# Value projections in products of 512 columns, cosine products into the rotated tiles, and four smaller moves, in a two-layer streaming encoder

## The chip, the cores and the metric

The kernel runs on one core of a Trainium2 chip. A core has a matrix engine (TensorE, PE in the profile; its weight loads are shown as PEld), a vector engine (VectorE, DVE), an activation engine (ScalarE, ACT), a general engine (GpSimd, POOL) and a queue that issues transfers (SyncE, SP). Each takes its instructions in the order in which they were written for it. Products are summed in eight banks of PSUM, each of 512 float32 columns in 128 partitions; everything else stands in SBUF or in HBM.

The metric is the device time of one execution in microseconds, as the median of several runs. Lower is better.

## The reference, cut to what matters

The input is one sequence of 1024 tokens of width 1024, float32. Layer 0 normalises, projects once, and runs two branches; layer 1 is a convolution module.

```
x = x + mixer_ab(rmsnorm(x))        # layer 0
x = x + mixer_conv(rmsnorm(x))      # layer 1
return rmsnorm(x)

mixer_ab(h):
    u, g_s5, q, k, v, g_ret = split(h @ w_in)       # 1024, 1024, 512, 512, 1024, 1024
    y_s5 = s5(u);  y_s5 = y_s5' * sigmoid(y_s5' @ glu_w + glu_b), y_s5' = gelu(y_s5)
    y_ret = retention(q, k, v)
    return concat(y_s5 * silu(g_s5), y_ret * silu(g_ret)) @ w_out

retention: 8 heads, key width 64, value width 128
    q, k = rope(q) / 8, rope(k)      # [x1 cos - x2 sin, x1 sin + x2 cos]
    scores = (q k^T) * decay mask, within chunks of 64
    out = scores v + (decayed q) S,  S = decayed sum of k v^T over earlier chunks
    out = normalised over each head's 128 columns

mixer_conv(h):
    a, b, g = split(h @ w_in)
    u = depthwise conv (31 taps) of a * sigmoid(b);  u = silu(layernorm(u)) * silu(g)
    return u @ w_out
```

## The kernel before

Activations are kept transposed: 128 features in the partitions, tokens along the free side, in halves of 512 tokens (`h` 0 and 1). To keep float32's accuracy each operand is split into a high and a low part of the type float32r. A block of eight feature tiles is then 8 x 3 products (`mm3`, lines 141 to 148): high weights by high data, high weights by low data, low weights by high data. The weights' high part is a cast on ACT (line 137), the low part a subtraction on POOL (line 138). Weights are fetched in one fixed sequence (`plan`), two ahead (`wnext`), in three buffers each for the raw, high and low parts. The weights that are used once for each half of the tokens write their low part to HBM the first time (line 112) and read it back the second time (`wload_again`, lines 115 to 124).

The data operands of a stage lie in two sets of 16 tiles, `A0` for the first half and `A1` for the second (pool `opA`). The next stage's operands take the same tiles as soon as their last reader is done.

Retention goes by pairs of heads (`retention`, line 802). For each pair `ret_proj` projects keys and queries (`project`, line 830), each as two products of 24 instructions into one of three projection banks, evacuated by DVE with the norm's factor into the tile `raw`. `turn` (line 840) rotates: four transfers exchange the 32-row blocks of `raw` into `swp`; POOL multiplies `raw` by the cosines and `swp` by the sines, both in place; DVE sums them into the rotated tile. Only the keys of pair 2 are projected ahead, before pair 1's heads.

Values have the tokens as rows, so here the data are the stationary operand and the weights are streamed. Pair 0 computes those of pairs 0 and 1 together, in products of 512 columns (`ret_values_wide`, line 887): for each half four banks (from the five auxiliary ones) are filled side by side while four pieces of the weights go by, so that each piece is loaded twice. Pairs 2 and 3 each compute their own, in products of 256 columns, one bank of 128 tokens after another (`ret_values`, line 868), with two pieces of weights.

`ret_heads` (line 909) transposes the rotated keys (`ktp`, then `kt` on DVE), forms the states (`kv`, `S`), the scores (`sp`), their masked copy (`sc`, line 959) and the output products (`ro`), takes each head's mean and variance (the root on ACT, `last_rs`), and transposes back (`rt`). Beside the retention, `y_pass` (line 779) fetches the state-space branch's output, applies Gelu on ACT and writes it to HBM (`yn_d`); the two passes of a pair stand behind the roots of the pair before on ACT. After pair 3 the GLU (lines 1055 to 1075) loads `yn_d` back (`yf`) and splits it into `yh` and `yl` (`split`, line 1016). The subtractions of the second half stand behind pair 3's `kt` on DVE.

In layer 1 the gates `silu(g)` are written to HBM (`gs_d`) and read back in `conv_norm` (line 1279, tile `gl`). The last stage, `w_out_c`, multiplies by the last weights (`woc`), adds the residual, and `final_norm` needs the sum of squares over all eight blocks (`token_sums`), its root, and a product that spreads it to all partitions (`spread`). The second half's last three blocks are done in quarters of 256 tokens; the last block's second quarter, and what follows it, is issued behind the spread of the first quarter (line 1392).

The program is written in the order of these stages, but the order on each engine is chosen beforehand by a planner that simulates the program: among what is ready it takes the lowest priority number (`at`). `issue_after(x)` keeps what is written in its block behind `x` on x's engine. So the heads of one pair are mixed with the projections of the next.

Of the kernel before, what the change touches and what calls it, by code (L numbers as in the profile page):

```python
# [11 lines left out]
F32 = mybir.dt.float32  # L12
# [26 lines left out]

class Trunk:  # L40
# [22 lines left out]
    def plan(self):  # L63

        A = self.A
        seq = [(A["w_ab"][nb], f"u{nb}") for nb in range(8)]
        seq += [(A["w_ab"][nb], f"g{nb}") for nb in range(8, 24)]
        for p in range(4):
            seq += [(A["w_ab"][28 + p], f"k{p}"), (A["w_ab"][24 + p], f"q{p}")]

            if p == 0:
                seq += [(A["w_v"][j], f"v{p}_{h}_{j}") for h in range(2) for j in range(4)]
            elif p > 1:
                seq += [(A["w_v"][2 * p + i], f"v{p}_{i}") for i in range(2)]
# [12 lines left out]
        seq += cg(1, range(G0))  # L87
        seq += [(A["w_out_c"][nb], f"woc{nb}_{h}") for h in range(2) for nb in range(8)]
        self.wseq, self.wissued, self.wgot = seq, {}, 0
        self.wnames, self.lo_d = {n for _, n in seq}, {}  # L90
# [24 lines left out]
    def wload_again(self, src, name, low):  # L115
        nc = self.nc
        wf = self.wp.tile([P, D], F32, name=f"wf_{name}", tag="wf", bufs=3)
        wh = self.wp.tile([P, KB, P], F32R, name=f"wh_{name}", tag="wh", bufs=3)
        wl = self.wp.tile([P, KB, P], F32R, name=f"wl_{name}", tag="wl", bufs=3)
# [3 lines left out]
        nc.sync.dma_start(wl[:].rearrange(fl).bitcast(F32), low)  # L123
        return wh, wl
# [663 lines left out]
    def retention(self, st):  # L788
# [13 lines left out]
        for pair in range(4):  # L802
            cur = list(ahead or self.ret_proj(pair))[-1]

            ahead = pair == 1 and self.ret_proj(pair + 1)
            if ahead:
                next(ahead)
            if pair == 0:
                V = self.ret_values_wide()
            elif pair > 1:  # L810
                V = self.ret_values(pair)
            with ExitStack() as held:
                if pair:
                    held.enter_context(self.tc.issue_after(self.last_rs.ins))
                for cb in (2 * pair, 2 * pair + 1):
                    self.y_pass(rq, cb)

            def turned():
                if pair == 3:
                    early.close()  # L820
                    self.lp = self.pool("l1", side="right")
            self.ret_heads(pair, *cur, V, turned)

    def ret_proj(self, pair):
# [5 lines left out]
        def project(nm):  # L830
            w = self.wnext(f"{nm}{pair}")
            raw = raws[nm] = self.rq.tile([P, T], F32, name=f"{nm}raw_{pair}", tag="raw", bufs=2)
            for h in range(2):
# [3 lines left out]
                last = nc.vector.tensor_tensor(raw[:, c], ps[:], self.R[:, c], op=ALU.mult)  # L837
            return last

        def turn(nm, behind=None):  # L840
# [27 lines left out]
    def ret_values(self, pair):  # L868

        nc = self.nc  # L870
        wv = [self.wnext(f"v{pair}_{i}") for i in range(2)]
        vt = self.rp.tile([P, 8, 256], F32, name=f"v_{pair}", tag="v", bufs=2)
        for b in range(8):
            ps = self.bank(f"mm_v{pair}_{b}", aux=False)
            h, o = b // 4, (b % 4) * P
            for kb in range(KB):
                xh, xl = self.xs[h][kb]
                i, k4 = kb // 4, kb % 4
                wh = wv[i][0][:].rearrange("p (k a) n -> p k (a n)", a=2)[:, k4, :]
                wl = wv[i][1][:].rearrange("p (k a) n -> p k (a n)", a=2)[:, k4, :]  # L880
                nc.tensor.matmul(ps[:, :256], xh[:, o:o + P], wh, start=kb == 0, stop=False)
                nc.tensor.matmul(ps[:, :256], xh[:, o:o + P], wl, start=False, stop=False)
                nc.tensor.matmul(ps[:, :256], xl[:, o:o + P], wh, start=False, stop=kb == KB - 1)
            nc.scalar.mul(vt[:, b, :], ps[:, :256], self.Rtok[:, b:b + 1])
        return lambda p, b, hh: vt[:, b, hh * P:(hh + 1) * P]

    def ret_values_wide(self):

        nc = self.nc
        res = []  # L890
        for h in range(2):
            vt = self.rp.tile([P, 4, HALF], F32, name=f"v_0_{h}", tag="v", bufs=2)
            pss = [self.bank(f"mm_v0_{h}_{b}") for b in range(4)]
            for j in range(4):
                wh, wl = (t[:].rearrange("p (k a) n -> p k (a n)", a=4) for t in self.wnext(f"v0_{h}_{j}"))
# [11 lines left out]
        return lambda p, b, hh: res[b // 4][:, b % 4, (2 * p + hh) * P:(2 * p + hh + 1) * P]  # L907

    def ret_heads(self, pair, K, Q, qadds, V, turned):
# [39 lines left out]

        sc = [rp.tile([P, 8, P], F32, name=f"sc{hh}_{pair}", tag=f"sc{hh}", bufs=1) for hh in range(2)]  # L950
        for hf in range(2):
# [6 lines left out]
            for hh in range(2):  # L958
                v.tensor_tensor(sc[hh][:, 4 * hf:4 * hf + 4, :], sps[hh][:].rearrange("p (b i) -> p b i", b=4),
                                self.mask[:, 2 * pair + hh, :].unsqueeze(1).broadcast_to([P, 4, P]), op=ALU.mult)  # L960
# [60 lines left out]
    def layer0_back_and_layer1(self, st):  # L1021
# [217 lines left out]
        def conv_norm(h):  # L1239
# [26 lines left out]
            for nb in range(8):  # L1266
# [12 lines left out]
                nc.sync.dma_start(g[:], self.gs_d[rows(nb), hs(h)])  # L1279
# [71 lines left out]
        for h in range(2):  # L1351
# [31 lines left out]
            with self.at(430000):  # L1383
                last = [w_out_c(h, nb, quarters) for nb in (5, 6, 7)]
# [4 lines left out]
                after = self.last_spread  # L1389
# [40 lines left out]
def layout(inp):  # L1430
# [10 lines left out]
    wv = w[:, 3072:4096].reshape(2, 4, P, 4, 256)  # L1441
    A["w_v"] = wv.transpose(3, 0, 2, 1, 4).reshape(8, P, KB, P)
    A["w_v"][:4] = w[:, 3072:3584].reshape(4, 2, P, HALF).transpose(0, 2, 1, 3).reshape(4, P, KB, P)
# [49 lines left out]
```

## Time and profile before

| | |
|---|---|
| median of 3 runs | 1215.66 us (1213.5 to 1219.05) |
| profiled execution | 1212.99 us, span of the profile 1211.2 us |
| TensorE clock granted, mean | 0.997 |
| PE busy | 1195.8 us, 99% of the span |
| DVE, POOL, ACT busy | 62%, 55%, 40% |
| value products of 512 columns, pairs 0 and 1 | 192, from 359.3 to 402.8 us |
| value products of 256 columns, pair 2 and pair 3 | 192 each, from 470.2 and from 529.5 us |
| GLU's first product | 553.3 us |

All times inside the profile are counted from the start of the span. A row of the timeline gives the start, the duration, the engine, the line, the operation with output and inputs, how many were merged and, in brackets, the idle time before it and what ended it. Matmuls overlap in the pipeline: the duration of one is longer than the distance to the next, and the distance is what a product costs.

### The profile page before, as it was taken

What the parts mean: (1) busy time and instruction counts of PE and PEld (TensorE: products, weight loads), DVE (VectorE), ACT (ScalarE), POOL (GpSimd) and SP (SyncE); (2) the same over time, 40 slices, a digit from 0 to 9 for tenths busy, and PEclk for the clock granted to TensorE, in tenths of its full rate; (3) what the DMA queues carried; (4) which work ended last, traced back from release to release, by engine and by line L of the source; (5) the groups of instructions that cost most, each with busy time, mean ns of one, the idle gap of its engine ahead of it and who ended that gap; (6) DMA issues with size and microseconds to landing.
All of it is one profiled execution on the core that took longest, in us unless ns stands there. A gap on an engine that the chain in (4) does not pass through costs nothing.

```text
span 1211.2 us, 17238 instructions
## 1 busy us (share of the span) xinstructions
PE 1195.8 (99%) x6468; PEld 1001.7 (83%) x6468; DVE 748.2 (62%) x1337; ACT 479.9 (40%) x706; POOL 664.0 (55%) x457
## 2 busy tenths in 40 slices
PE   9999999999999999999999999999999999999997
PEld 7888888888888889998888888888888788888876
DVE  7965655555412457457547102699999699899533
ACT  7212232332223233144335322545535575434652
POOL 2059988888237253253453651678453567758642
PEclk9999999999999999999999999999999999999998
DMA  9342433333385166467446877765667654356664
GB/s 334 105 140 72 140 129 132 128 128 139 110 284 177 53 208 160 155 208 256 143 158 223 285 272 250 243 209 208 212 241 256 222 192 152 123 176 240 237 254 149
DMA packets 100227, 227.11 MB, mean 188 GB/s; under 512 B 9264, under 2 KB 38192, under 8 KB 99504
## 3 DMA queue, kind: packets, MB, share of 16 engines
q1 hardware_dynamic: 100144, 226.01, 55.1%
q8 instruction: 51, 0.84, 0.3%
q14 instruction: 32, 0.26, 0.1%
HBM read 160.51 MB, written 61.28 MB: 183 GB/s over the span
## 4 chain that ended last, share of the span: by engine, by line
PE 94%; DMA 2%; ACT 2%; DVE 1%; issue 0%; SPq 0%; POOL 0%; DVEq 0%
PE mm_g L148 7%; PE mm_g L147 7%; PE mm_g L146 7%; PE mm_wo L148 5%; PE mm_wo L146 5%; PE mm_wo L147 5%; PE mm_a L148 2%; PE mm_b L147 2%; PE mm_b L148 2%; PE mm_a L146 2%; PE mm_a L147 2%; PE mm_b L146 2%; PE mm_u L148 2%; PE mm_u L147 2%; PE mm_u L146 2%; PE mm_glu L146 2%
## 5 line engine op out<-in xcount | busy, mean ns | idle before, releaser
L1194 DVE SCALAR_TENSOR_TENSOR cv<-u,convw,cv 128x512 f32<-128x512 f32 x398 | 273.5, 752 | 11.9 <-ACT cv L1180 9.6
L1174 POOL TENSOR_TENSOR tp<-tp,tp 128x512 f32<-128x512 f32 x64 | 82.9, 1296 | 45.5 <-ACT tp L1173 44.4
L148 PE MATMUL mm_g<-xh,wl_g 128*128 128x512 f32 x256 | 100.8, 394 | 0.0
L147 PE MATMUL mm_g<-xl,wh_g 128*128 128x512 f32 x256 | 100.6, 393 | 0.0
L146 PE MATMUL mm_g<-xh,wh_g 128*128 128x512 f32 x256 | 100.5, 393 | 0.0
L1173 ACT ACTIVATE tp<-u,convw 128x512 f32<-128x512 f32 x64 | 45.7, 719 | 35.6 <-POOL tp L1174 33.9
L329 DVE TENSOR_TENSOR gt<-mm_g,R 128x512 f32<-128x512 f32 x32 | 21.9, 686 | 60.0 <-PE mm_g L148 60.0
L138 POOL TENSOR_TENSOR wl_v<-wf_v,wh_v 128x1024 fp32r<-128x1024 f32 x12 | 29.0, 2425 | 51.9 <-ACT wh_v L137 51.9
L147 PEld LDWEIGHTS mm_g<-xl,wh_g 128*128 128x128 f32 x256 | 48.1, 188 | 11.3 <-issue 1.6
L148 PEld LDWEIGHTS mm_g<-xh,wl_g 128*128 128x128 f32 x256 | 48.0, 188 | 10.6
L146 PEld LDWEIGHTS mm_g<-xh,wh_g 128*128 128x128 f32 x256 | 48.1, 188 | 9.6
L148 PE MATMUL mm_oc<-zh,wl_woc 128*128 128x512 f32 (+1 forms) x152 | 54.3, 360 | 1.0 <-DMA wl_woc<-lo_woc 1.0
L1094 DVE TENSOR_TENSOR x<-mm_wo,xr 128x512 f32<-128x512 f32 x16 | 11.1, 691 | 70.3 <-PE mm_wo L148 39.6
L147 PE MATMUL mm_oc<-zl,wh_woc 128*128 128x512 f32 (+1 forms) x152 | 53.9, 357 | 0.6 <-POOL zl L1019 0.6
L146 PE MATMUL mm_oc<-zh,wh_woc 128*128 128x512 f32 (+1 forms) x152 | 54.3, 363 | 0.0
L1066 POOL TENSOR_TENSOR yg<-yg,yn 128x512 f32<-128x512 f32 x16 | 22.5, 1404 | 53.5 <-DMA yg<-gs_d 15.6
L148 PE MATMUL mm_a<-h1h,wl_ca 128*128 128x512 f32 x128 | 50.3, 393 | 1.1 <-DMA wl_ca<-lo_ca 1.1
L147 PE MATMUL mm_u<-xl,wh_u 128*128 128x512 f32 x128 | 50.1, 391 | 1.0 <-DVE xl L261 1.0
L146 PE MATMUL mm_g<-h1h,wh_cg 128*128 128x512 f32 x128 | 50.4, 394 | 0.0
L146 PE MATMUL mm_glu<-yh,wh_glu 128*128 128x512 f32 x128 | 50.3, 393 | 0.0
L146 PE MATMUL mm_b<-h1h,wh_cb 128*128 128x512 f32 x128 | 50.2, 392 | 0.0
L146 PE MATMUL mm_wo<-yrh,wh_wor 128*128 128x512 f32 x128 | 50.2, 392 | 0.0
(400 smaller groups left out, 3624.3 us busy)
## 6 DMA issues: line engine op xcount, KB each, us to landing
wf_g<-w_ab SPq DMA_DIRECT2D x16, 512.0 KB, 4.0
wf_wos<-w_out SPq DMA_DIRECT2D x16, 512.0 KB, 5.5
wf_wor<-w_out SPq DMA_DIRECT2D x16, 512.0 KB, 5.8
wf_cb<-w_c SPq DMA_DIRECT2D x16, 512.0 KB, 4.5
wf_ca<-w_c SPq DMA_DIRECT2D x16, 512.0 KB, 4.7
wf_woc<-w_out_c SPq DMA_DIRECT2D x16, 512.0 KB, 5.2
wf_v<-w_v SPq DMA_DIRECT2D x12, 512.0 KB, 4.5
wf_cg<-w_c SPq DMA_DIRECT2D x11, 512.0 KB, 4.0
```

Of the source, the lines that this page charges most:

```text
L138: lo[i].tensor_tensor(wl[:].rearrange(fl)[:, c], wf[:, c], h.bitcast(F32), op=ALU.subtract)
L146: nc.tensor.matmul(ps, wh[:, kb, :], xh, start=start, stop=False)
L147: nc.tensor.matmul(ps, wh[:, kb, :], xl, start=False, stop=False)
L148: self.last_mm = nc.tensor.matmul(ps, wl[:, kb, :], xh, start=False, stop=stop)
L329: nc.vector.tensor_tensor(gt[:, c], ps[:], self.R[:, c], op=ALU.mult)
L1066: gp.tensor_tensor(yg[:], yg[:], yn[:], op=ALU.mult)
L1094: v.tensor_tensor(t[:], ps[:], xt[:], op=ALU.add)
L1173: nc.scalar.mul(sk[:], u[:, k:k + HALF], cw[:, nb, k:k + 1])
L1174: gp.tensor_tensor(s0[:], s0[:], sk[:], op=ALU.add)
L1194: v.scalar_tensor_tensor(dst[:], *tap, accs_[i][:], op0=ALU.mult, op1=ALU.add)
```

## The change

Seven things, in the order of the program:

1. All values are computed by the wide form: pair 0 for pairs 0 and 1, pair 2 for pairs 2 and 3, in products of 512 columns. Pair 3 has no value products of its own. The weights' layout follows.
2. Three of the wide form's four banks are projection banks; the fourth is an auxiliary one.
3. The cosine product is written to the rotated tile, no longer over `raw`, both halves of it before the sine products; the sum is taken in place there.
4. In pair 3 keys and queries are projected by halves in turn: keys 0, queries 0, keys 1, queries 1. In the others keys come first, then queries.
5. The last two of the second half's subtractions for the GLU (`kb` 6 and 7) stand behind the masked scores of pair 3's first half of tokens instead of behind `kt`.
6. The first two gate loads of `conv_norm(0)` are issued behind the second read of the low part of the weights `ca1`; the low parts of `woc3` and `woc4`, second reading, go to four tiles of the set `A1` instead of two of the three weight buffers.
7. In the last quarter the last block's products are no longer all behind the spread of the quarter before: the first nine stand behind its sums, the rest behind its spread.

```
+class Halves:
+    def __init__(self, tiles):
+        self.tiles = [t[:].rearrange("p (k n) -> p k n", k=KB // 2) for t in tiles]
+    def __getitem__(self, i):
+        p, kb, n = i
+        return self.tiles[kb // (KB // 2)][p, kb % (KB // 2), n]
 # plan
-            if p == 0:
-                seq += [(A["w_v"][j], f"v{p}_{h}_{j}") for h in range(2) for j in range(4)]
-            elif p > 1:
-                seq += [(A["w_v"][2 * p + i], f"v{p}_{i}") for i in range(2)]
+            if p % 2 == 0:
+                seq += [(A["w_v"][2 * p + j], f"v{p}_{h}_{j}") for h in range(2) for j in range(4)]
 # wload_again
+        if name in ("woc3_1", "woc4_1"):
+            tiles = [self.op_tile(self.opA, "A1", f"wl{i}_{name}") for i in range(2)]
+            for i, t in enumerate(tiles):
+                nc.sync.dma_start(t[:].bitcast(F32), low[:, i * HALF:(i + 1) * HALF])
+            return wh, Halves(tiles)
+        wl = self.wp.tile([P, KB, P], F32R, name=f"wl_{name}", tag="wl", bufs=3)
+        self.low_load[name[:-2]] = nc.sync.dma_start(wl[:].rearrange(fl).bitcast(F32), low)
 # retention
-            if pair == 0:
-                V = self.ret_values_wide()
-            elif pair > 1:
+            if pair % 2 == 0:
                 V = self.ret_values(pair)
 # ret_proj: project yields after each half
             for c in cs:
-                nc.gpsimd.tensor_tensor(raw[:, c], raw[:, c], tab[:, 0, c], op=ALU.mult)
+                nc.gpsimd.tensor_tensor(o[:, c], raw[:, c], tab[:, 0, c], op=ALU.mult)
+            for c in cs:
                 nc.gpsimd.tensor_tensor(swp[:, c], swp[:, c], tab[:, 1, c], op=ALU.mult)
-            return o, [lambda c=c: nc.vector.tensor_tensor(o[:, c], raw[:, c], swp[:, c], op=ALU.add) for c in cs]
-        project("k")
+            return o, [lambda c=c: nc.vector.tensor_tensor(o[:, c], o[:, c], swp[:, c], op=ALU.add) for c in cs]
+        k, q = project("k"), project("q")
+        for step in ((k, q, k) if pair == 3 else (k, k)):
+            next(step)
         yield None
         krot, adds = turn("k")
-        last = project("q")
+        for last in q:
+            pass
 # ret_values, the form of 256 columns, is removed; ret_values_wide takes its name
-            pss = [self.bank(f"mm_v0_{h}_{b}") for b in range(4)]
+            pss = [self.bank(f"mm_v{pair}_{h}_{b}", aux=b == 3) for b in range(4)]
 # ret_heads
+                self.masked[hf] = v.tensor_tensor(sc[hh] ... mask ..., op=ALU.mult)
 # load_split
-                self.split(f, a, b, v, None if halves or h == 0 else self.last_kt)
+                self.split(f, a, b, v, None if halves or h == 0 else self.last_kt if kb < 6 else self.masked[0])
 # conv_norm
-                nc.sync.dma_start(g[:], self.gs_d[rows(nb), hs(h)])
+                with self.tc.issue_after(self.low_load["ca1"].ins) if h == 0 and nb < 2 else nullcontext():
+                    nc.sync.dma_start(g[:], self.gs_d[rows(nb), hs(h)])
 # the last quarters
-                last = [w_out_c(h, nb, quarters) for nb in (5, 6, 7)]
+                among = {}
+                last = [w_out_c(h, nb, quarters, among) for nb in (5, 6, 7)]
...
-                with self.tc.issue_after(after.ins):
-                    next(last[2])
-                    final_norm(1, quarters[1])
+                among.update({0: sums, 3: spread})
+                next(last[2])
+                final_norm(1, quarters[1])
```

More of the change, by code (lines that the diff above doesn't have):

```diff
@@ L836, in project @@
                 self.gemm(ps[:], w, self.xs[h])
-                last = nc.vector.tensor_tensor(raw[:, c], ps[:], self.R[:, c], op=ALU.mult)
-            return last
+                yield nc.vector.tensor_tensor(raw[:, c], ps[:], self.R[:, c], op=ALU.mult)
         def turn(nm, behind=None):
@@ L870, in ret_values @@
         nc = self.nc
[L871 to L889, printed above, removed]
         res = []
         for h in range(2):
-            vt = self.rp.tile([P, 4, HALF], F32, name=f"v_0_{h}", tag="v", bufs=2)
-            pss = [self.bank(f"mm_v0_{h}_{b}") for b in range(4)]
+            vt = self.rp.tile([P, 4, HALF], F32, name=f"v_{pair}_{h}", tag="v", bufs=2)
+            pss = [self.bank(f"mm_v{pair}_{h}_{b}", aux=b == 3) for b in range(4)]
             for j in range(4):
-                wh, wl = (t[:].rearrange("p (k a) n -> p k (a n)", a=4) for t in self.wnext(f"v0_{h}_{j}"))
+                wh, wl = (t[:].rearrange("p (k a) n -> p k (a n)", a=4) for t in self.wnext(f"v{pair}_{h}_{j}"))
                 for b in range(4):
@@ L958, in ret_heads @@
             for hh in range(2):
-                v.tensor_tensor(sc[hh][:, 4 * hf:4 * hf + 4, :], sps[hh][:].rearrange("p (b i) -> p b i", b=4),
-                                self.mask[:, 2 * pair + hh, :].unsqueeze(1).broadcast_to([P, 4, P]), op=ALU.mult)
+                self.masked[hf] = v.tensor_tensor(
+                    sc[hh][:, 4 * hf:4 * hf + 4, :], sps[hh][:].rearrange("p (b i) -> p b i", b=4),
+                    self.mask[:, 2 * pair + hh, :].unsqueeze(1).broadcast_to([P, 4, P]), op=ALU.mult)
         gts = []
```

11 lines of the change are left out of this document (5 added, 6 removed).

## The prediction

> **What bounds the kernel now.** I read the page's busy times first, then the chain that ended last, then TensorE's waits, then the timelines of the stages that the diff touches.
>
> ```profile
> PE 1195.8 (99%) x6468; PEld 1001.7 (83%) x6468; DVE 748.2 (62%) x1337; ACT 479.9 (40%) x706; POOL 664.0 (55%) x457
> PE 94%; DMA 2%; ACT 2%; DVE 1%; issue 0%; SPq 0%; POOL 0%; DVEq 0%
> PE ro L979 <- DVE sc L959: 1.7, 1, 1.7
> PE rf_R L422 <- ACT x L1309: 1.2, 1, 1.2
> PE mm_a L148 <- DMA wl_ca<-lo_ca: 1.1, 1, 1.1
> PE mm_oc L148 <- DMA wl_woc<-lo_woc: 1.0, 2, 0.7
> ```
>
> The first line is busy time by engine, the second the chain's shares, the rest the waits of TensorE (PE) that bear on the change: total, times, longest. PE is the bound over the whole span; work on another engine costs only where PE then stands still. So I list what PE can lose: the products themselves, and the gaps. A busy PE is not one at its peak, so I took the distance between starts:
>
> ```profile
> 359.26 0.39 PE L901 MATMUL mm_v<-wh_v,xh 128*128 128x512 f32 x1
> 359.49 0.39 PE L902 MATMUL mm_v<-wl_v,xh 128*128 128x512 f32 x1
> 359.71 0.39 PE L903 MATMUL mm_v<-wh_v,xl 128*128 128x512 f32 x1
> ...
> 550.01 0.28 PE L881 MATMUL mm_v<-wh_v,xh 128*128 128x256 f32 x1
> 550.13 0.28 PE L882 MATMUL mm_v<-wl_v,xh 128*128 128x256 f32 x1
> 550.25 0.28 PE L883 MATMUL mm_v<-wh_v,xl 128*128 128x256 f32 x1
> ```
>
> A value product of 512 columns takes 0.2267 us from start to start, one of 256 columns 0.120, not 0.113. Subtracting these paces from all distances between starts leaves these gaps at places that the diff names: 1.87 + 0.28 at 564.5 and 566.7, 1.30 at 938.7, 0.84 at 1169.3, 1.34 at 1196.5. They lie here:
>
> ```profile
> 525.60 2.07 ACT L785 ACTIVATE yn<-yp 128x1024 f32<-128x1024 f32 x1 [4.95 <-DMA yp<-y_d]
> 564.86 0.69 DVE L1019 TENSOR_TENSOR yl<-yf,yh 128x512 fp32r<-128x512 f32 x1 [1.76 <-ACT yh L1017]
> 565.72 1.28 DVE L959 TENSOR_TENSOR sc<-sp,retmask 128x512 f32<-128x512 f32 x2
> 935.64 0.32 SPq L1279 DMA_DIRECT2D gl<-gs_d  x1
> 936.00 0.43 SPq L123 DMA_DIRECT2D wl_ca<-lo_ca  x1
> 940.27 0.50 PE L148 MATMUL mm_a<-h1h,wl_ca 128*128 128x512 f32 x1 [1.14 <-DMA wl_ca<-lo_ca]
> 1197.93 0.67 PE L422 MATMUL rf_R<-rf_dg,ones 128*128 128x256 f32 x2 [1.17 <-ACT x L1309]
> 1199.49 1.75 DVE L1330 TENSOR_TENSOR fo<-x,rf_R 128x256 f32<-128x256 f32 x5 [0.44 <-ACT RF L1320]
> ```
>
> The reader should see a queue blocked at its head twice: on DVE a split (yl) that waits for its input stands before the masked scores (sc) that PE wants, and on SP a load of a gate (gl) stands before the weights wl_ca.
>
> The profiled execution took 1212.99 us (span 1211.2), 2.7 below the median of the runs, 1215.66.
>
> **1. Values.** Removed: 2 x 192 products of 256 columns, 384 x 0.120 = 46.08. Added: 192 of 512, 192 x 0.2267 = 43.53. **-2.55 us**, all on PE. Also 8 evacuations of 0.69 on ACT for 16 of 0.47, and four more weight loads: each 512 KB of DMA, a 1.05 us cast on ACT, a 2.4 us subtraction on POOL. These are hidden by the products: the first pair's values load eight pieces in the same rhythm and PE lost nothing over their 192 products (-0.06). In 43.5 us POOL has 8 x 2.4 of subtractions and 8 x 1.3 of rotation, 30 in all; a piece that came late would cost its lateness, up to some 3 us.
> The Trainium skill (TensorE: Matmul & The Clock Gate, "Back-to-back issue gap") speaks against this term: it puts a warm product at N/2.4 + 2.5 ns, so two halves cost only 2.5 ns more than a whole and 192 pairs 0.5 us, an estimate from that page. The rows show 13 ns for a pair, and they decide.
>
> **2. Three projection banks.** The first value bank of a half is finished 18 products (4.1 us) before the half ends; its evacuation takes 0.69, and the next half's first product needs it. What could stand ahead of it on ACT is the Gelu with its table, 1.28 + 2.07 = 3.35. Together 4.04, just under; and no Gelu lies at either half's end (351 to 365 and 471 to 482, against ends near 381 and 492). Zero; ends 0 and 0.7. It frees auxiliary banks for the heads, whose gain is at most what PE lost there, nothing.
>
> **3. Cosine products.** They no longer overwrite raw, so POOL need not wait for the swap DMAs that read raw (16 issues of 0.59 on SP for keys, landing 4.5 to 8.3 us after issue); two products of 1.29 leave the chain from landing to rotated tile. The new wait is on the rotated tile's earlier readers, behind which POOL's weight subtractions would queue: pair 1's scores end at 460.4 and pair 2's key products now start at 463.4, so it costs nothing. In pairs 0 to 2 values or keys cover the rotation. 0 there.
>
> **4. The last pair.** This is the doubtful part. Its 23 us of values, which covered its rotation and the preparation of the GLU's operands, are now pair 2's. Heads 2 and pair 3's projections start 20.5 us later (43.5 - 23.0), at 515 for 495, and end near 550, where PE turns to the GLU 2.55 earlier than now. With keys and queries by halves (k0, q0, k1, q1) the first half's operands are free 10.9 us before that, about as now. It moves q0 before k1: the query weights are wanted 5.4 us sooner (their subtraction ran at 494.9, 20 us ahead), and the keys' four swap issues on SP and two sine products on POOL come 5.4 nearer the end, among yn_d's write, the yf loads and grl on SP and a GLU subtraction of 2.4 on POOL. But the last Gelu follows heads 2's roots: from root (516.0) to Gelu's end is 11.7 us, then yn_d's write 3.1, the load of yf 4.1, cast 0.62, split 0.69, so 20.2. Roots near 536.5 give 556.7; PE reaches that eighth block at 550 + 7 x 0.68 = 554.8, or 555.6 if the 0.8 us of transposes comes before. Late by 1 to 2 us. Keys: the second half ends near 543, evacuated 543.9, four issues, landing 6.4, two sine products 1.3 and 1.7, sums 1.8 and 0.7: rotated near 557. Queries, landing 4.0: near 562. Until then PE has two GLU blocks of 5.44 on first-half operands, transposes 0.8 and states 1.7, 13.4 us for a gap of 12: enough if the planner places them so. The second half's last two splits now wait for the first masked scores, so the 1.87 + 0.28 at 564.5 should go. I take 0.8 of new gaps against 2.15 old: **-1.3**; ends -2.15 and +4 (the lateness of keys and of the Gelu in full, less what is covered).
>
> **5. Gates behind wl_ca.** The load at 935.64 waited for a write to gs_d. Without it wl_ca can go when its sister was cast, 932.2, lands 4.3 later, 936.5, before 938.7. **-1.3**. The two moved gate loads are read at 994 and have 45 us. DVE's convolution is 97% busy between 1000 and 1050, and could take this back, but at 930 to 960 it is idle 7.7 of 30, waiting for this mm_a. Ends -1.3 and 0.
>
> **6. wl_woc.** Two weights go to other tiles, as four loads of 256 KB instead of two of 512; SP issues two more (0.4 each). They need not wait for the three wl buffers that were released at 1167. **-0.8**; ends -0.84 and 0.
>
> **7. The last block.** Nine of its products, 9 x 0.12 = 1.08, run between sums and spread, in the gap of 1.34. But its last sum on DVE then meets the row at 1199.49, five products of the earlier quarter that end 1201.24; the last sum came at 1201.50. If those keep their place only 0.26 is won. I take **-0.4**, nearer that row; ends -1.08 and 0.
>
> Sum: -2.55 -1.3 -1.3 -0.8 -0.4 = **-6.4** (1206.6 beside the profiled 1212.99). Taken from the median: 1209.3, I say 1209. All best ends give -7.9 (1207.7); all worst, a late value piece and bank with them, +5.2 (1220.8).
>
> **Rivals.**
> A: the last pair's cover is missed. Gaps of 3 to 5 instead of 0.8, gain 2 to 4: 1212.5. For it: the Gelu chain is late by the rows' own sums, and the order of issue is fixed beforehand while landings vary (2.5 to 7.6 for yn_d). Against: two ready GLU blocks.
> B: terms 5 to 7 are given back downstream, to the convolution on DVE or the closing products; gain 3.9: 1211.8. If halves cost 0.5 us in all and not 2.55, 4.3 is left, 1211.3; 0.03 of B, since the paces are measured. (This is the rule of the Trainium skill in part 1.)
> C, slower: last queries late. The split behind the masked scores makes GLU's second half depend on the query chain (swap, sine, sum, score, mask). If the planner sets those GLU products ahead of what is ready, all three projection banks wait for it: PE then goes bare through the heads, whose part from 552.5 to 586.2 holds 12 us of own work and 21 of GLU. It decides against the change from a loss of 6.4 + 1.3; ten to 15 us give 1213 to 1224, middle 1219.
> The change does what it says in all these.
>
> **Chances.** Under 0.5% (6.1 us) a measurement of this kernel can hardly tell from no change. Forecast 0.50 (own range 1206 to 1211, its upper part just within the bound); A 0.25, B 0.13, C 0.12. Giving C half to within: faster 0.49, within 0.43, slower 0.08. Range 1203 to 1217: run-to-run spread (1213.5 to 1219.05) below, A, B and the lighter half of C above.
>
> **What would show it.** Right: 192 value products of 512 columns at a pace of 0.227 in pair 2, none of 256; PE gaps of 0.8 us or less in all between 540 and 575; no wait on wl_ca or wl_woc; spread behind nine products, its wait under 0.4. Wrong: PE waiting for yh, yl, krot or qrot at 550 to 570; DVE's sums of the last block still behind fo; a wait on a value bank's evacuation at the middle of the values.

## The result, and the profile after

The forecast was 1209 us, 6.6 faster. The changed kernel is slower: 1223.2 us, median of 11 runs (1220.8 to 1225.1), beside 1217.65 for the kernel before on the same chips (11 runs, 1212.8 to 1221.1). The ratio is **1.0046, 95% interval 1.0033 to 1.0059**, some 5.6 us. The time lies outside the predicted range of 1203 to 1217.

The profiled execution of after took 1223.37 us (span 1221.5), 10.4 more than the profiled one of before. That one lies at the low end of its runs, so a difference of the two traces overstates the loss; I use the traces for where the time went, and the ratio for how much.

The page's busy line and the shares of the chain, after:

```profile
PE 1199.2 (98%) x6276; PEld 995.4 (81%) x6276; DVE 745.0 (61%) x1337; ACT 482.6 (40%) x702; POOL 673.8 (55%) x461
PE 91%; DMA 4%; DVE 2%; issue 2%; ACT 1%; POOL 1%; SPq 0%; DVEq 0%; POOLq 0%; ACTq 0%
```

192 instructions fewer, and yet 3.4 us more of busy time; PE's share of the chain fell from 94% to 91%. So PE stood still more often, and part of its work ran slower. What it waited for (total, times, longest):

```profile
PE mm_oc L164 <- DMA wl_woc<-lo_woc: 3.9, 2, 2.5
PE ktp L918 <- DVE krot L866: 2.0, 2, 1.1
PE mm_wo L164 <- POOL wl_wos L154: 1.6, 1, 1.6
PE ro L981 <- DVE sc L960: 1.5, 1, 1.5
...
PE sp L954 <- DVE qrot L866: 1.1, 2, 0.6
...
PE mm_wo L164 <- POOL wl_wor L154: 0.8, 1, 0.8
PE mm_wo L162 <- ACT wh_wor L153: 0.7, 1, 0.7
PE rf_ps L419 <- DVE fo L1334: 0.6, 1, 0.6
```

The wait on wl_ca is gone, the one on wl_woc has grown from 1.0 to 3.9 (1.4 of it at an earlier weight, at 1164), and the last pair of heads waits for its keys, its queries and its scores (ktp, sp, ro) where it waited for the scores alone. Three waits at the start of w_out are new.

Cut by five marks in PE's order, the 10.3 us between the two spans are these:

| stretch | before, us | after, us | difference |
|---|---|---|---|
| start to the first product of w_out | 655.00 | 659.87 | +4.87 |
| of it, up to the GLU's first product, less the 0.8 of transposes that lay before it in before | 552.53 | 550.48 | -2.05 |
| of it, from there to w_out | 102.47 | 109.39 | +6.92 |
| first w_out product to the spread of layer 1's norm | 97.15 | 101.58 | +4.43 |
| from there to the first product with woc | 348.54 | 347.08 | -1.46 |
| from there to the first product of 256 columns | 80.69 | 84.09 | +3.40 |
| from there to the end | 29.82 | 28.90 | -0.92 |

The values came as forecast. Their pace, in PE's timeline of after:

```profile
503.72 0.39 PE L903 MATMUL mm_v<-wh_v,xl 128*128 128x512 f32 x1
503.95 0.39 PE L902 MATMUL mm_v<-wl_v,xh 128*128 128x512 f32 x1
504.18 0.39 PE L903 MATMUL mm_v<-wh_v,xl 128*128 128x512 f32 x1
```

0.227 us from start to start. The loss begins behind them, in the last pair. Gaps of PE above 0.2 us between the GLU's first product and w_out, found as in the prediction, sum to 6.46 (ktp 1.02 and 1.27, sp 0.65 and 0.81, ro 1.67 and smaller ones) against 2.15 before. The SyncE queue and then VectorE's timeline in that stretch:

```profile
546.97 2.44 SPq L859 DMA_DIRECT2D kswp<-kraw  x4
549.91 0.33 SPq L802 DMA_DIRECT2D yn_d<-yn  x1
...
553.66 2.12 SPq L1050 DMA_DIRECT2D yf<-yn_d  x2
555.87 2.42 SPq L859 DMA_DIRECT2D qswp<-qraw  x4
```

```profile
555.58 3.43 DVE L866 TENSOR_TENSOR krot<-krot,kswp 128x512 f32<-128x512 f32 x2 [2.47 <-POOL kswp L865]
562.50 0.69 DVE L1021 TENSOR_TENSOR yl<-yf,yh 128x512 fp32r<-128x512 f32 x1 [3.50 <-ACT yh L1019]
563.11 1.28 DVE L920 TENSOR_TENSOR kt<-ktp,kdec 128x512 f32<-128x512 f32 x2
...
569.52 0.68 DVE L866 TENSOR_TENSOR qrot<-qrot,qswp 128x512 f32<-128x512 f32 x1
...
576.19 2.48 DVE L1021 TENSOR_TENSOR yl<-yf,yh 128x512 fp32r<-128x512 f32 x1 [0.56 <-ACT yh L1019]
578.59 0.68 DVE L960 TENSOR_TENSOR sc<-sp,retmask 128x512 f32<-128x512 f32 x1
579.83 1.74 DVE L1073 SCALAR_TENSOR_TENSOR sg<-sg,yg 128x512 f32<-128x512 f32 x1 [0.56 <-POOL yg L1068]
581.49 0.68 DVE L960 TENSOR_TENSOR sc<-sp,retmask 128x512 f32<-128x512 f32 x1
```

The queries' swap stands on SP behind two loads of yf that wait for the last Gelu's write, and goes out at 555.9; the queries are rotated at 570.2. On VectorE `kt` stands behind a late yl, though the transposes it reads were done at 559.8, and the second pair of masked scores stands behind another yl and a sigmoid product.

### The profile page after: what moved, and what is told of

The parts are those of the page before. It is cut to its first block, busy times and chain, and to the rows that moved or that the text cites. A ratio compares the mean times of both kernels' runs of the same rounds, so it can differ in the third digit from the quotient of the medians.

```text
span 1221.5 us, 16884 instructions
## 1 busy us (share of the span) xinstructions
PE 1199.2 (98%) x6276; PEld 995.4 (81%) x6276; DVE 745.0 (61%) x1337; ACT 482.6 (40%) x702; POOL 673.8 (55%) x461
## 4 chain that ended last, share of the span: by engine, by line
PE 91%; DMA 4%; DVE 2%; issue 2%; ACT 1%; POOL 1%; SPq 0%; DVEq 0%; POOLq 0%; ACTq 0%
PE mm_g L163 7%; PE mm_g L164 7%; PE mm_g L162 7%; PE mm_wo L164 4%; PE mm_wo L163 4%; PE mm_wo L162 4%; PE mm_b L164 2%; PE mm_v L901 2%; PE mm_b L162 2%; PE mm_v L902 2%; PE mm_a L164 2%; PE mm_b L163 2%; PE mm_a L162 2%; PE mm_v L903 2%; PE mm_a L163 2%; PE mm_u L164 2%
## 5 line engine op out<-in xcount | busy, mean ns | idle before, releaser
L154 POOL TENSOR_TENSOR wl_v<-wf_v,wh_v 128x1024 fp32r<-128x1024 f32 x16 | 40.9, 2561 | 32.9 <-ACT wh_v L153 32.9
L163 PEld LDWEIGHTS mm_g<-xl,wh_g 128*128 128x128 f32 x256 | 48.1, 188 | 11.3 <-issue 1.6
L164 PE MATMUL mm_wo<-ysh,wl_wos 128*128 128x512 f32 x128 | 49.9, 390 | 1.6 <-POOL wl_wos L154 1.6
L163 PE MATMUL mm_glu<-yl,wh_glu 128*128 128x512 f32 x128 | 50.8, 397 | 0.0
L164 PE MATMUL mm_wo<-yrh,wl_wor 128*128 128x512 f32 x128 | 50.0, 391 | 0.8 <-POOL wl_wor L154 0.8
L164 PE MATMUL mm_glu<-yh,wl_glu 128*128 128x512 f32 x128 | 50.4, 395 | 0.0
```

Of the source, the lines that this page charges most:

```text
L154: lo[i].tensor_tensor(wl[:].rearrange(fl)[:, c], wf[:, c], h.bitcast(F32), op=ALU.subtract)
L163: nc.tensor.matmul(ps, wh[:, kb, :], xl, start=False, stop=False)
L164: self.last_mm = nc.tensor.matmul(ps, wl[:, kb, :], xh, start=False, stop=stop)
```

## Experiments

All ratios are to the kernel before, timed on the same chip. "Last pair" is the sum of PE's gaps above 0.2 us from the GLU's first product to w_out: 2.15 us in before, 6.46 in after.

**1. The values alone, undone and done.** Theory T says that the loss comes of the 23 us of values which no longer cover the last pair. First the kernel after with narrow values again:

```
 # plan, retention, ret_values, the weights' layout: as before the change
-            if pair % 2 == 0:
+            if pair == 0:
+                V = self.ret_values_wide(pair)
+            elif pair > 1:
                 V = self.ret_values(pair)
```

> The changed kernel with part 1 alone undone: pairs 2 and 3 compute their own values again in products of 256 columns; every other part stays. Theory T (the loss comes with the values that left pair 3, which covered its rotation and the GLU's operands): the gaps between 550 and 585 us shrink from some 8 us to 2 or less, w_out starts without its 4.4 us of gaps, and the time is below the kernel before, ratio 0.995 to 0.999. Rival R (the loss comes from another part: halves in turn, the split behind the masks, the moved loads): the gaps stay, ratio 1.004 to 1.009, slower than the changed kernel by the 2.6 us of the narrow products.

Then the kernel before with the wide values and nothing else (all four banks auxiliary):

```
-            if pair == 0:
-                V = self.ret_values_wide()
-            elif pair > 1:
-                V = self.ret_values(pair)
+            if pair % 2 == 0:
+                V = self.ret_values_wide(pair)
```

> The kernel before with part 1 alone done: values of pairs 2 and 3 in products of 512 columns, with the four auxiliary banks that pair 0 had. Theory T: as slow as the changed kernel or slower, since what shortens the last pair's chain is missing, ratio 1.004 to 1.010. Rival R: the products' 2.6 us are won, ratio 0.997 to 0.999.

Measured: narrow again 1215.54 us, ratio 1.0016 (1.0001 to 1.0032); wide alone 1227.82, ratio 1.0114 (1.0087 to 1.0140). The last pair's gaps are 1.73 us in the first; in the second 6.56, with a further 4.65 at 470.7 in pair 1's heads. PE's waits, narrow again and then wide alone:

```profile
PE mm_oc L166 <- DMA wl_woc<-lo_woc: 2.5, 2, 2.2
...
PE ro L1004 <- DVE sc L983: 1.0, 2, 0.8
```

```profile
PE rt L1003 <- DVE on L995: 4.5, 1, 4.5
PE sp L949 <- DVE qrot L847: 2.8, 2, 1.7
PE mm_glu L144 <- ACT yh L1013: 2.5, 1, 2.5
```

The loss comes with the wide values, and T holds for the place. From the GLU to the spread of layer 1's norm the wide kernel loses nearly as much as after does: 5.9 us up to w_out and 4.3 behind it, beside 6.9 and 4.4. The 4.65 in pair 1's heads after does not have; no run says which part of the change removes it. T's time for the narrow kernel, below the kernel before, did not come. The other parts lessen the loss (1.0114 to 1.0046) but win nothing by themselves (1.0016), where the forecast gave them 3.8 us. The first of the two fences shows one reason: the wait on wl_woc has stayed.

**2. Which link in the last pair: the late y?** The kernel after, where the GLU's blocks 6 and 7 read rows 4 and 5 of the state-space branch, which are there early (so the GLU multiplies other data):

```
                         f = f2[:, kb % 2, :]
-                        nc.sync.dma_start(f, src[rows(kb), hs(h)])
+                        nc.sync.dma_start(f, src[rows(kb - 2 if kb > 5 else kb), hs(h)])
```

> The changed kernel, but the GLU's splits for feature tiles 6 and 7 read tiles 4 and 5 of the Gelu's output, which are written earlier; the GLU's input is thus partly another one. Theory G (the last Gelu's tiles come late; their split stands ahead of kt on DVE and holds the heads of pair 3): heads 3 end 3 to 6 us earlier, ratio 0.9995 to 1.002. Rival K (the keys' swap alone holds the heads): at most 1 us earlier, ratio 1.0035 to 1.005.

Measured: 1219.44 us, ratio 1.0032 (1.0014 to 1.0050). The keys' waits are gone and the queries are rotated at 566.4 instead of 570.2, yet the last transposes of the heads end only 0.7 us earlier. That is not G's 3 to 6 us; it is the size that K gave, but not K's cause, since the keys wait no more. One wait holds what two held:

```profile
PE ro L981 <- DVE sc L960: 3.4, 1, 3.4
```

From 573.9 PE waits for the second pair of masked scores, which VectorE starts at 576.8, behind the two yl that the change had put between the two pairs of scores and behind a sigmoid product; last pair 6.08. The late y is one head of a queue; behind it stands the next.

**3. The start of w_out.** The kernel after, where w_out reads pair 2's retention rows in place of pair 3's (so a quarter of its retention operand is other data):

```
                     if halves:
                         f = lp.tile([P, HALF], F32, name=f"{name}f{kb}_{h}", tag="tp", bufs=3)[:]
-                        nc.sync.dma_start(f, src[rows(kb), hs(h)])
+                        nc.sync.dma_start(f, src[rows(kb - 2 if kb > 5 else kb), hs(h)])
```

> The changed kernel, but the splits of the retention's output for the last product read pair 2's rows in place of pair 3's, which are written some 45 us earlier; the product's input is thus partly another one. Theory W (the gaps of 4.4 us at the start of w_out come from pair 3's rows, which heads 3 hand over 11 us later): these gaps go, time 3 to 5 us below the changed kernel, ratio 1.0005 to 1.002. Rival P (the low parts of the weights are late on POOL by themselves): the gaps stay, ratio 1.004 to 1.005.

Measured: 1220.5 us, ratio 1.0055 (1.0038 to 1.0071). In the trace the gaps at the start of w_out fall from 3.91 us (1.74, 0.86, 0.38, 0.93) to 1.27, so the late rows made two thirds of them: pair 3's heads end 11 us later than in before, ACT's casts of their rows wait for the loads, and the casts of the weights stand behind those. ACT's timeline of after, ahead of the gap of 1.74 at 673:

```profile
669.21 0.62 ACT L1019 CAST yrh<-yrf 128x512 fp32r<-128x512 f32 x1 [4.19 <-DMA yrf<-yr_d]
669.74 1.05 ACT L153 CAST wh_wos<-wf_wos 128x1024 fp32r<-128x1024 f32 x1
```

The time itself does not show it: the ratio is not W's (1.0005 to 1.002) but lies above P's. The last pair of this execution loses 0.8 us more in its larger gaps, and the interval of the ratio spans 4 us, more than the 2.6 in question, and overlaps that of after. Shown in the place, not in the total.

**4. wl_woc: the order on SP.** The kernel after with the two weights back in the common buffers:

```
-        if name in ("woc3_1", "woc4_1"):
-            tiles = [self.op_tile(self.opA, "A1", f"wl{i}_{name}") for i in range(2)]
...
-            return wh, Halves(tiles)
```

> The kernel after with the two low weights woc3_1 and woc4_1 back in the buffers of the others, each loaded in one piece; everything else as after. Theory P (order on SP): in after, the four halves stand on SP behind the load of woc5_1, which waits for a buffer that TensorE releases at 1167; in the old order the wait on wl_woc in the output phase is 0.8 us, as in the kernel before, in place of 2.64, and the stretch at half pace after it (1180 to 1185) is gone with it. Gain over after: 1.8 to 3.4 us, a ratio to the kernel before of 1.002 to 1.003. Rival Q (the wait is the landing time of the loads, whatever their order, or comes of the work arriving later than in before): the gap stays at 2.2 or more and the ratio at 1.004 to 1.006.

Measured: 1217.63 us, ratio 1.0022 (1.0002 to 1.0042), in the range that P gave, though its interval overlaps that of after (1.0033 to 1.0059). In after the halves were written behind the load of woc5_1, and SP stands there 6.5 us for a buffer that PE releases. SP's timeline of after, then PE's:

```profile
1163.25 5.31 SPq L1298 DMA_DIRECT2D x1l<-x_d  x3
1174.87 0.32 SPq L139 DMA_DIRECT2D wl_woc<-lo_woc  x1
1175.24 1.85 SPq L136 DMA_DIRECT2D wl_woc<-lo_woc  x4
```

```profile
1177.17 0.40 PE L163 MATMUL mm_oc<-zl,wh_woc 128*128 128x512 f32 x1
1180.03 0.50 PE L164 MATMUL mm_oc<-zh,wl_woc 128*128 128x512 f32 x1 [2.47 <-DMA wl_woc<-lo_woc]
```

L139 is woc5_1, L136 the four halves: free tiles, at a blocked place in the queue. With the move undone the gap is 0.75 (0.84 in before), and the stretch at half pace behind it does not come (below).

**5. The parts without the values, in the right order.** The kernel before with the gates behind wl_ca, the new tail, and the halves of woc3 and woc4, now issued ahead of woc5_1. Parts 6 and 7 are as in the change; the order is new:

```
+            self.low_half = nc.sync.dma_start(t[:].bitcast(F32), low[:, i * HALF:(i + 1) * HALF])
...
+        with self.tc.issue_after(self.low_half.ins) if name == "woc5_1" else nullcontext():
+            self.low_load[name[:-2]] = nc.sync.dma_start(wl[:].rearrange(fl).bitcast(F32), low)
```

> The kernel before with only three parts of the change: the gates behind wl_ca, the closing block's products among the last sums, and the two low weights on the other tiles, here with the load of woc5_1 issued behind their halves. Values, projections, rotation and the last pair are those of before. Theory (the gain of these parts does not hang on the values): wl_ca's wait goes (1.3 to 1.45), the wait on wl_woc falls from 0.84 to under 0.3 once the halves are not behind a load that waits, the tail gives 0.26: 2.0 to 2.5 us, a ratio of 0.998 to 0.9985. Rival B (given back later to the convolution or the closing products, or the wait on wl_woc stays above 0.8 whatever the order): under 1 us, ratio 0.999 to 1.001.

Measured: 1213.33 us against 1213.74, ratio 0.9993 (0.9974 to 1.0013). The trace shows all three gains: to woc 347.24 (before 348.54), to the first product of 256 columns 79.73 (80.69), to the end 28.65 (29.82); 3.4 us in all. SP's timeline, with the first half out 7.3 us ahead of woc5_1's load:

```profile
1161.05 1.85 SPq L138 DMA_DIRECT2D wl_woc<-lo_woc  x4
...
1168.32 0.38 SPq L142 DMA_DIRECT2D wl_woc<-lo_woc  x1
```

The gap at wl_woc is gone altogether, not only back to 0.8. This execution's own other gap (1.30 before sp at 458, which before's trace does not have) took part of it back. The ratio lies in rival B's range and not in the theory's; 12 runs between 1208 and 1218 do not tell 2 to 3 us from none.

**6. Can the wide values be mended?** First the last Gelu passes moved into pair 2, the rest as after:

```
-                for cb in (2 * pair, 2 * pair + 1):
+                for cb in ((0, 1), (2, 3), (4, 5, 6, 7), ())[pair]:
                     self.y_pass(rq, cb)
```

> The kernel after with the last two Gelu passes of y (those that followed heads 2's roots) issued with the two before them, so that no root, Gelu, write of y or load of yf lies between 515 and 560. Theory G (what is late behind the last pair's projections is held by the late y: SP by the yf loads that wait for it, VectorE by the split of yf): queries are rotated near 566 and not 570.2, keys' product waits less than 0.5 us, the second half's scores come near 574 and not 581.5, the gaps between 555 and 600 fall from 8 us to 4, and the last yr rows are 4 us earlier, so that the gaps of 4.4 at the start of w_out halve. Gain over after 3 to 6 us, ratio 1.000 to 1.002. Rival K (the chain of the queries alone: evacuation, swap, sums): the queries' rotation ends within 2 us of after's and the gaps with it; gain under 2 us, ratio 1.003 to 1.005. A cost of its own would show in pair 2's stage, 470 to 516, where four passes now meet the values' weights on ScalarE: products of the values waiting for wh.

Measured: 1218.69 us, ratio 1.0032 (1.0010 to 1.0054); last pair 1.67, and gaps of 0.38 and 0.95 left at w_out's start. So G was right on the place, while the time lies in K's range. The passes meet the values' weights on ACT, and one product waits:

```profile
490.30 1.85 PE L901 MATMUL mm_v<-wh_v,xh 128*128 128x512 f32 x5 [2.55 <-ACT wh_v L153]
```

Then with the order of woc mended too, and four of the second half's splits behind the second pair of scores:

```
-                self.split(f, a, b, v, None if halves or h == 0 else self.last_kt if kb < 6 else self.masked[0])
+                self.split(f, a, b, v, None if halves or h == 0 else self.last_kt if kb < 4 else self.masked[1])
```

> The kernel after with three things mended: the last two passes of y issued with the two before them; the second half's splits for blocks 4 and 5 as well as 6 and 7 placed behind the second pair of masked scores; the load of woc5_1 issued behind the halves of woc3_1 and woc4_1. Theory T with G and P (all that the wide values cost is the last pair's missed cover, VectorE's and SP's queues there, and the order of one load): the gaps between 555 and 600 fall from 8 us to about 3, the gaps at w_out's start from 4.4 to 2, the wait on wl_woc from 2.64 to 0.3: 6 to 9 us under after, a ratio of 0.997 to 0.999, which would beat both kernels. Rival K (with the queries' rotation as last link, some 5 us of gaps remain wherever the splits stand, and splits that are later hold the GLU's own products): ratio 1.000 to 1.003. A wait of the GLU's products on yh or yl between 575 and 597 would be the sign of the second half of K.

Measured: 1215.47 us, ratio 1.0006 (0.9992 to 1.0020), the best with wide values and level with the kernel before, where theory T had it beat both; last pair 3.29. Its largest waits:

```profile
PE mm_oc L165 <- DMA wl_woc<-lo_woc: 1.4, 1, 1.4
PE sp L955 <- DVE qrot L867: 1.4, 2, 0.8
PE mm_wo L165 <- DMA wl_wos<-lo_wos: 1.3, 1, 1.3
```

The wait on wl_woc is the one at an earlier weight (here at 1157); none is left behind the moved halves.

**7. The Gelu passes dealt out 3, 3, 2, 0.** On the narrow kernel of experiment 5, and the same with three of the six closing products of the earlier quarter behind the last sum:

```
-                for cb in (2 * pair, 2 * pair + 1):
+                for cb in ((0, 1, 2), (3, 4, 5), (6, 7), ())[pair]:
# the second one also:
+                with self.tc.issue_after(late.ins) if late and e is v else nullcontext():
                     e.tensor_tensor(o[:, nb % 2, :], t[:, c], (R if e is gp else rp)[:, :n], op=ALU.mult)
```

> The kernel with the small parts (e8_small) and, besides, the eight Gelu passes of y dealt out 3, 3, 2 and 0 to the four pairs of heads instead of 2 each, so that none is left for the last pair. Theory G for the kernel before as well (the gap of 1.87 us behind the last pair's scores is VectorE held by the split of a late yf): the gap before ro at 565 falls under 0.4 us and no new one comes; 1 to 1.9 us under e8_small in the trace, a ratio of 0.9965 to 0.9985. Rival (passes moved ahead meet the values' weights on ScalarE, as the pass at 487 did with four passes in pair 2, 2.71 us there): a new wait of 0.9 us or more on a value product in 350 to 500, ratio 0.999 to 1.000.

> As e10_small_y, and three of the six products of the closing block's first quarter that VectorE does (fo) are put behind the last sum of the second quarter. Theory (part 7 won 0.26 and not 0.4 to 1.08 since VectorE does those products ahead of the last sum): TensorE's wait rf_ps <- fo of 0.81 us goes, and 0.5 to 0.8 us of the span with it. Rival (the products put back delay the reciprocal or the last store): the wait on rf_R grows from 1.34 by as much, no gain.

Measured: 1224.33 us, ratio 1.0066 (1.0050 to 1.0081), and 1224.44, ratio 1.0069 (1.0057 to 1.0080). Both theories fell, and neither rival's mark came. A third pass in pair 1 puts a write of yn_d (444.83) and a load of y ahead of the queries' swap on SP. The swap on SP without the third pass (experiment 5), then SP and PE with it:

```profile
444.04 2.42 SPq L864 DMA_DIRECT2D qswp<-qraw  x4
```

```profile
446.54 2.76 SPq L864 DMA_DIRECT2D qswp<-qraw  x4
```

```profile
461.79 2.08 PE L977 MATMUL sp<-qrot,krot 64*128 64x128 f32 x16 [4.99 <-DVE qrot L870]
465.77 0.55 PE L977 MATMUL sp<-qrot,krot 64*128 64x128 f32 x1 [1.90 <-DVE qrot L870]
```

2.5 us later at the queue became 6.4 at the rotated queries (first half 461.6 for 455.2), and gaps of 5.16 and 2.21 us. The swap lands 8.5 to 9.1 us after its issue for 3.8 to 4.8 without the pass, with other loads on their way; no run varied those alone. And the gap before ro did not go (0.95 and 2.29). With y early the yf loads still go out late, one by one as their buffers come free (the one for the first of these gaps at 568.4, landing 5.4 us later), and at the second it is the sigmoid's table and product that stand ahead of the scores.

In the second kernel the last sum does come first, at once when its product ends, but PE waits longer. VectorE, then PE:

```profile
1210.83 0.42 DVE L1331 TENSOR_TENSOR x<-mm_oc,x1l 128x256 f32<-128x256 f32 x1 [0.53 <-PE mm_oc L167]
1211.17 1.07 DVE L1361 TENSOR_TENSOR fo<-x,rf_R 128x256 f32<-128x256 f32 x3
```

```profile
1212.38 1.12 PE L422 MATMUL rf_ps<-ones,s2q 128*128 128x64 f32 x8 [1.60 <-DVE fo L1361]
```

rf_ps begins when the last fo has ended (1212.24), though the squares of the last block were there at 1211.7. It waits for what fo reads, which fits a PSUM bank shared by the spread and the next sums; I did not try other banks. So in these traces fo first was the better order, and the new wait of after (rf_ps <- fo, 0.6) is no sign of a late sum.

**8. Wide against narrow, both mended alike but for the last pair's order.**

> The same mends as e11_small_y_tail on the kernel after (with its wide values, halves, and the second half's splits from block 4 on behind the second masked scores). It sets the wide values against the narrow ones with nothing else between them but the last pair's order. Theory T (the cover that the narrow values give the last pair is worth about what the wide products save): within 1.5 us of e11_small_y_tail, either side, with 1.5 to 3 us of gaps in 555 to 600 where that has under 0.5. Rival W (once y is early, the wide values keep their 2.55 us): 1.8 to 2.6 us under e11_small_y_tail, a ratio to the kernel before of 0.994 to 0.996.

Its diff to after is that of e9_wide_mended with the passes and the tail of experiment 7. Measured: 1220.29 us, ratio 1.0033 (1.0017 to 1.0049), 0.36% less than the narrow kernel with the same mends. By that comparison neither theory's number came: the wide form loses less to the third pass (gaps of 2.10 and 1.76 at 456 to 459, for 3.69 and 2.20), so the pair is no clean test of the cover. The better pair is e9_wide_mended and e8_small, timed on one chip, each with the passes where they did least harm: 1.0006 and 0.9993, with overlapping intervals.

**9. Halves or not.** The kernel after with all the keys before the queries in pair 3:

```
-        for step in ((k, q, k) if pair == 3 else (k, k)):
+        for step in (k, k):
```

> The kernel after with the last pair's projections in the old order, both halves of the keys and then both of the queries; the rest as after. Theory (halves are worth something once the values are gone, since the first half's queries are there earlier): 2 to 5 us slower than after, ratio 1.006 to 1.009, with the queries rotated at 572 or later. Rival (the halves' order is itself a cause of the loss, since the keys' second swap and the queries' come together on SP behind the yf loads): keys rotated before 552, no wait at ktp, the queries no later than 571, and 1 to 3 us faster than after, ratio 1.002 to 1.004.

Measured: 1226.72 us, ratio 1.0093 (1.0075 to 1.0112); last pair 10.04 for 6.46. By the gaps the halves are worth 3.6 us once the values are gone, by the two ratios 5.7, a little over the theory's 2 to 5; though not by the last queries (568.1, for 570.2 with halves): the first half's queries were evacuated at 549.0 and not 540.0, and PE waits 4.5 us for the scores at ro, 3.3 of it at once. The loss has about the theory's size without its mark (queries at 572 or later); the rival fell.

## Why the prediction was wrong

**Values, -2.55: right.** 2.05 less at the GLU's first product, with all products at the forecast pace. The Trainium skill (TensorE: Matmul & The Clock Gate, "Back-to-back issue gap") would have given 0.5 for the two halves of each product; the trace decides for the row.

**The last pair, -1.3 with ends of -2.15 and +4: the step that failed.** "13.4 us for a gap of 12: enough if the planner places them so" rested on keys at 557, queries at 562 and the last Gelu's yl at 556.7. The keys came at 559.0, the yl at 563.2 and the queries at 570.2. Three terms of the queries' chain were too small. The second half of the queries was evacuated at 553.1, 2.5 us after its products, behind other work on VectorE. Its swap was issued at 555.9 to 558.3, behind the yf loads on SP: the prediction named these loads and gave them no time. It landed 6 us later, not 4. The fill was there, but not in the gaps: PE had GLU products left, and they stood behind the link that waited.

The old gap was read rightly as a split in front of the masked scores, and before the first scores it went (0.23 left of 1.87 + 0.28). But the two splits, moved behind the first scores, now stood in front of the second, where 1.67 came. Nor is the last Gelu alone what makes the split late: in experiment 7 y is early, the yf loads wait for their buffers, and 0.95 stays.

Measured +6.9 at equal work: 4.3 of gaps above 0.2 us, 1.4 at half pace at 560, 1.2 more at half pace at 580 (last section).

**What is late next, not asked: +4.4.** The heads end 11 us later (597.1 for 586.2), so pair 3's rows reach w_out late. The prediction followed the chain to the scores and stopped. Experiment 3 shows the place and two thirds of the gaps.

**Gates behind wl_ca, -1.3: right.** -1.46; every kernel that has it takes 347.1 to 347.3 in this stretch, the two that have not 348.5 (before) and 348.2 (e2_wide_only), and nothing is given back to the convolution.

**wl_woc, -0.8 with ends of -0.84 and 0: wrong sign, +3.4.** "They need not wait for the three wl buffers" is true of the tiles and false of the queue: SP had a load that does wait in front of them. All six kernels with that order lose 1.4 to 3.4 in this stretch, four of them partly at half pace. With that load behind them five kernels gain 0.2 to 1.0 (-0.96 in experiment 5).

**The last block, -0.4: right in kind.** -0.92 here, near the best end of -1.08, but one execution does not size it: other kernels with this tail take 28.65 to 29.71 us for the stretch, and e2_wide_only, with the old one, 29.50. The sum does stand behind fo, as forecast. The gap of 1.34 before the first spread is gone, and 0.2 of it has come back before the last.

Of the rivals, A had the place (the cover missed) with gaps of 3 to 5 where 6.5 came, and no part downstream. C had the queries late and a loss of ten to 15 us, of which 11.3 came (6.9 and 4.4), and the measured time lies in its 1213 to 1224. But the way was another: PE was not out of GLU products in the heads (it did 108 of them before the last transposes, 81 in before), it waited at each link. B did not happen. The sum -6.4 became +10.3 in the traces and about +5.6 in the medians.

## What to carry to other kernels

When work is moved away, list every queue's instructions in the place that it leaves, with what each waits for, and take the one at the head as the time of all behind it; then ask what the end of that place feeds. A load into a free buffer is early only if nothing that waits is issued before it on the same queue. A few us of products beside a chain of transfer, sum and mask were worth about as much here as a form that saves 5% of those products (experiment 8).

## What was not expected of the hardware

At some gaps the granted clock of PE falls to a half, for 3.4 us or a multiple of it. PE's timeline of after behind the gaps of 1.02 and 1.27 us:

```profile
560.49 0.63 PE L162 MATMUL mm_glu<-yh,wh_glu 128*128 128x512 f32 x1
560.91 0.63 PE L163 MATMUL mm_glu<-yl,wh_glu 128*128 128x512 f32 x1
...
563.04 0.39 PE L162 MATMUL mm_glu<-yh,wh_glu 128*128 128x512 f32 x1
563.27 0.39 PE L163 MATMUL mm_glu<-yl,wh_glu 128*128 128x512 f32 x1
```

Windows (times, length, busy time and instructions by engine, then the granted clock, the DMA share and GB/s), three of after and then one of e4_no_late_y:

```profile
560.00:563.00 3.00, 3.00 (x8) 2.31 (x7) 0.50 (x1) 1.15 (x3) 0.00 (x0) 0.50 1.00 259
580.10:583.50 3.40, 3.40 (x19) 3.18 (x16) 3.40 (x12) 0.00 (x0) 0.92 (x1) 0.50 1.04 384
1180.00:1184.00 4.00, 3.97 (x11) 3.20 (x12) 0.87 (x2) 1.44 (x3) 0.00 (x0) 0.60 1.02 390
576.40:583.20 6.80, 5.71 (x31) 5.49 (x32) 6.80 (x32) 0.60 (x2) 0.78 (x1) 0.50 0.69 269
```

0.427 us from start to start, then 0.227 again: seven products and 1.4 us at 560 and as much at 1181. At 580 it meets the output products (ro) of the last pair and costs 1.7 us, 0.5 of it counted among the gaps. A half clock came with gaps of 1.67 and 2.64 us (after), 2.41 (e7_early_y, e3_no_halves) and 3.61 (e4_no_late_y), and with two gaps of 2.3 in sum (after). It did not come with gaps of 2.39 (e1_narrow), 2.41 (e4_no_late_y, at 1178) or 2.68 us (e2_wide_only, at 567). So a gap of two to four us costs itself, and in some executions 1.4 to 1.7 us more, and executions of one kernel differ in it: of the twelve of e12_wide_y_tail the four with a mean granted clock of 0.995 or more took 1216.9 to 1218.1 us, the four with 0.991 or less 1221.5 to 1225.4. The Trainium skill (TensorE: Matmul & The Clock Gate, "What's actually happening") has a clock gate with a free-running window that halves the rate after an idle one; that the same length of gap does or does not bring it fits such a window. Its advice to avoid idle gaps above some 3 us ("Why this matters for your kernels") is too lax for these rows: one gap of 1.67 us, or 2.3 in two pieces, was enough. No run here varied one gap alone, so the threshold stays open.
